# Decode index scores: keys as the moving side, queries as 32 weight columns, four matmuls on the four quarters of the array's columns

## The chip, the core and the metric

The kernel runs on one core of a Trainium2 chip. The metric is device time in microseconds (us) of one execution; lower is better. The engines of the core have these names in the profile: PE (TensorE, matmuls; PEld is its weight loads), DVE (VectorE), ACT (ScalarE), POOL (GpSimd) and SP (SyncE, which issues most DMAs). Each works through its own queue in order; semaphores tie them together.

## What is computed

One inference step of a hybrid decoder layer: a prompt of 1024 tokens and 8 decode sequences of one token each go through a common input projection, a sparse-attention head group, an mLSTM head group and an output projection. The change is in the sparse attention of the decode sequences. Each has 4096 past tokens in 32 pages of 128, scattered in a pool by a page table. An indexer scores every past key (64 numbers) against 16 query heads, and the best 256 tokens are then attended to:

```python
def indexer_scores(qi, ki, wi):
    s = jax.nn.relu(jnp.einsum('bqhd,bld->bqlh', qi, ki))
    return jnp.einsum('bqlh,bqh->bql', s, wi) * IDX_SCALE

def dsa_sample(q, k_new, v_new, qi, ki_new, wi, cache_k, cache_v, cache_ik, page_table):
    ki_past = cache_ik[page_table].reshape(Bd, past, IDX_DIM)
    ki_all = jnp.concatenate([ki_past, ki_new], axis=1)
    scores = indexer_scores(qi, ki_all, wi)
    ...
    _, idx = lax.top_k(scores, topk)
```

All in fp32. Only the order of the scores matters afterwards, so the kernel leaves the constant scale out.

## The kernel before

The kernel is one long stream of projection matmuls on PE, with everything else woven into it. The projections (`proj`, `mm` at L1410; `vproj` at L1479 and L1484) are computed in fp32r, each product split into high and low parts: three matmuls for one. Weights arrive as `wraw`, ACT casts the high part (L216, L1474) and DVE subtracts to get the low part (L217, L1475).

The other work is cut into jobs, Python generators that stand in two lanes (L1360). After each piece of a projection `lane.step` lets each lane advance; what a job `yield`s is a cost, and the lane spreads a job's total cost over the time up to the job's due end. So the yields set between which projection matmuls a job's instructions are written. A scheduler may then move instructions, except those that `pin` keeps in the order of the program. Every engine runs its queue in the order that comes out.

`job_dscore` is the first job of lane 1 and runs beside `vproj`, beside the first projections after it and beside lane 0's prompt indexer (`job_index`, L490 to L505). Its parts:

- The pool of indexer keys, `cik`, is laid out as rows (page, group of 4 dimensions), 2 KB each: 4 dimensions of 128 tokens. A gather (`fetch`, L996, an indirect DMA issued by POOL) brings 8 pages: partition 16g+q holds dimensions 4q to 4q+3 of page g. There are 4 gathers per batch, 32 in all, with 3 buffers `kp`. `idx` (L989) holds the row numbers.
- For each batch DVE builds `bd` (L1011): the queries, times a mask that is one only where page and column group agree.
- PE multiplies (L1016): weights are `kp[:, r, :]` (128 x 128 tokens), the moving side is `bd[:, r]` (128 columns: 8 pages by 16 heads), summed over r = 0 to 3. Four of these per gather, 16 per batch, 128 in all, fp32. The result has tokens on partitions and (page, head) on columns, in one bank for a batch's 32 pages.
- DVE applies relu and the head weights (`wib`) in one instruction (L1019) and adds over the 16 heads (L1021) into `sD`: token in page by (batch, page).
- At the end eight small matmuls (L1024) score the new keys.

`job_dsel` picks the best 256 from `sD`, and `job_datt` gathers and attends. PSUM has eight banks: three for the projections (`psj`), five that all others share (`bank()`).

Of the kernel before, what the change touches and what calls it, by code (L numbers as in the profile page):

```python
# [79 lines left out]
def constants():  # L80
# [8 lines left out]
    c[:, C_P64] = p % 16  # L89
# [52 lines left out]
def body(tc, A, stop=None):  # L142
# [830 lines left out]
    def job_dscore():  # L973
        with tc.tile_pool(name="ds", bufs=2, side="right") as pd:
            iqr = pd.tile([128, 4, 16, NB], F32, name="iqr", bufs=1)
            iqs = pd.tile([64, 16, NB], F32, name="iqs", bufs=1)
            g8 = pd.tile([128, 8], F32, name="g8", bufs=1)
            SY.dma_start(g8, A["cst"][:, C_G8:C_G8 + 8])
            wib = pd.tile([128, 16, NB], F32, name="wib", bufs=1)
            idx = pd.tile([128, 32], I32, name="idx", bufs=1)  # L980
            pte = pd.tile([128, 32], I32, name="pte", bufs=1)
            pin(SY.dma_start(pte, A["pte"]))
# [6 lines left out]
            pin(V.tensor_scalar(idx, pte, 16.0, cst[:, C_P64:C_P64 + 1], OP.mult, OP.add))  # L989
            V.memset(sD, NEG)  # L990
            kps = []

            def fetch(m):
                if m < NB * 4:
                    kp = pd.tile([128, 4, 128], F32, name="kp", bufs=3)
                    pin(G.indirect_dma_start(out=kp.rearrange("p r k -> p (r k)"), out_offset=None, in_=A["cik"],  # L996
                                             in_offset=bass.IndirectOffsetOnAxis(ap=idx[:, m:m + 1], axis=0)))
                    kps.append(kp)

            fetch(0)  # L1000
            yield 4
            fetch(1)
            yield 4
            for b in range(NB):
                ps = bank()
                for c in range(4):
                    fetch(b * 4 + c + 2)
                    if not c:
                        yield 2
                        bd = pd.tile([128, 4, 8, 16], F32, name="bd", bufs=1)  # L1010
                        pin(V.tensor_tensor(bd, iqr[:, :, :, b].unsqueeze(2).to_broadcast([128, 4, 8, 16]),  # L1011
                                            g8.unsqueeze(1).unsqueeze(3).to_broadcast([128, 4, 8, 16]), OP.mult))
                    yield 4 if c else 2
                    kp = kps.pop(0)
                    for r in range(4):
                        PE.matmul(ps[:, c * 128:c * 128 + 128], kp[:, r, :], bd[:, r].rearrange("p g h -> p (g h)"),  # L1016
                                  start=(r == 0), stop=(r == 3))
                tm = pd.tile([128, NPG, 16], F32, name="tm", bufs=1)
                V.scalar_tensor_tensor(tm, ps.rearrange("p (a h) -> p a h", h=16), 0.0,  # L1019
                                       wib[:, :, b].unsqueeze(1).to_broadcast([128, NPG, 16]), OP.max, OP.mult)  # L1020
                V.tensor_reduce(sD[:, b, 0:NPG], tm, AX.X, OP.add)  # L1021
            pn = bank()
            for b in range(NB):
                PE.matmul(pn[0:1, b * 16:b * 16 + 16], dec[0:64, T_MISC, b:b + 1], iqs[:, :, b], start=True, stop=True)  # L1024
# [377 lines left out]
    def mm(ps, cols, t, q, c, H, L, between={}):  # L1402
        c0, cn = chunks(t)[c]
        for k in range(4):
# [4 lines left out]
            for w_, x_, z in ((H, xH, 0), (H, xL, 1), (L, xH, 2)):  # L1409
                m = PE.matmul(ps[:cols, :cn], w_[:, k, :cols], x_[kk][:, c0:c0 + cn],  # L1410
                              start=(kk == 0 and z == 0), stop=(kk == 15 and z == 2))
                if k in between and z == 0:
                    pin(m)
# [362 lines left out]
```

## Time and profile before

| | |
|---|---|
| median of 3 runs | 2025.92 us (2025.28 to 2028.26) |
| the profiled execution | 2025.66 us, of which span 2023.9 us |
| granted TensorE clock, mean | 0.998 |
| decode score job, first and last matmul (L1016) | 203.8 and 418.6 us |

The span is the profiled part of an execution. In the lines below a group reads: line, engine, operation, output<-inputs by the program's names, shape, count, then durations. In a view of one line or tile the three numbers are least, median and greatest duration in ns, and the two after them the first and last start in us. In the timeline the two leading numbers are start and duration in us, and square brackets give the idle time of the engine just before and what ended it. A window row gives, for a stretch of time, each engine's busy time and instruction count, then the granted clock of PE, the DMA engines' busy share and GB/s. Matmuls are pipelined, so the records of PE overlap one another.

### The profile page before, as it was taken

The page shows a single profiled execution, that of the slowest core. Times are in us where ns is not written, and L with a number is a line of the kernel's source. Part 1 is how long each engine was busy: PE and PEld are TensorE (multiplying, and loading weights), DVE is VectorE, ACT ScalarE, POOL GpSimd, SP SyncE. Part 2 cuts the span into 40 slices and gives each one's busy share as a digit, 9 for nine tenths or more (in the row PEclk, how much of TensorE's full clock was granted, in tenths as well). Part 3 has the DMA queues.
Part 4 walks back from the last instruction along what each step waited for, and adds up shares of the span by engine and source line. Part 5 has one row for each costly group of instructions (what it writes and reads, how often), then busy time and mean ns, then how long its engine had stood idle before and what let it go on. Part 6 is the DMA issues. An engine that isn't in the chain of part 4 may idle for free.

```text
span 2023.9 us, 33968 instructions
## 1 busy us (share of the span) xinstructions
PE 2012.4 (99%) x12378; PEld 1925.2 (95%) x12378; DVE 1209.5 (60%) x3011; ACT 823.3 (41%) x1729; POOL 230.9 (11%) x295
## 2 busy tenths in 40 slices
PE   9999999999999999999999999999999999999998
PEld 9998999999999999999999999999999999988886
DVE  8333467756685876887455555436878556654332
ACT  8123345333531455312355555435555344423222
POOL 0000111100000000023110011012222211101110
PEclk9999999999999999999999999999999999999999
DMA  7444645432222212254422332145776658566212
GB/s 254 112 118 136 181 133 150 128 97 85 78 72 72 79 48 63 68 157 142 126 69 79 115 95 88 45 131 169 224 224 193 163 194 303 169 239 209 84 47 104
DMA packets 202004, 265.25 MB, mean 131 GB/s; under 512 B 33541, under 2 KB 128965, under 8 KB 201837
## 3 DMA queue, kind: packets, MB, share of 16 engines
q1 hardware_dynamic: 196589, 248.99, 40.2%
q0 software_dynamic: 4096, 12.59, 2.1%
q8 instruction: 97, 1.59, 0.3%
q10 hardware_dynamic: 1152, 1.51, 0.2%
q14 instruction: 70, 0.57, 0.1%
HBM read 203.19 MB, written 59.82 MB: 130 GB/s over the span
## 4 chain that ended last, share of the span: by engine, by line
PE 99%; issue 1%; DMA 0%; ACT 0%; DVE 0%; POOLq 0%; POOL 0%; SPq 0%; ACTq 0%
PE pj L1410 56%; PE bank L1601 7%; PE bank L1639 6%; PE pj L1639 4%; PE pj L1479 3%; PE bank L490 3%; PE pj L1484 3%; PE bank L686 3%; PE bank L635 3%; PE bank L1479 2%; PE bank L1410 2%; PE bank L677 2%; PE bank L1016 1%; PE bank L889 1%; PE bank L1484 1%
## 5 line engine op out<-in xcount | busy, mean ns | idle before, releaser
L1410 PE MATMUL pj<-xH,wH 128*128 128x344 f32 (+1 forms) x2352 | 759.6, 325 | 1.8 <-ACT xH L271 0.7
L1410 PE MATMUL pj<-xL,wH 128*128 128x344 f32 (+1 forms) x2352 | 761.1, 324 | 0.0
L1410 PE MATMUL pj<-xH,wL 128*128 128x344 f32 (+1 forms) x2352 | 758.7, 323 | 0.0
L1410 PEld LDWEIGHTS pj<-xH,wH 128*128 128x128 f32 x2352 | 443.0, 189 | 4.7 <-ACT xH L271 1.2
L1410 PEld LDWEIGHTS pj<-xL,wH 128*128 128x128 f32 x2352 | 443.0, 188 | 2.2 <-DVE xL L272 0.3
L1410 PEld LDWEIGHTS pj<-xH,wL 128*128 128x128 f32 x2352 | 443.3, 189 | 1.7
L216 ACT CAST wH<-wraw 128x512 fp32r<-128x512 f32 (+1 forms) x343 | 209.4, 615 | 515.2 <-PE pj L1410 313.1
L217 DVE TENSOR_TENSOR wL<-wraw,wH 128x512 fp32r<-128x512 f32 (+1 forms) x343 | 243.0, 715 | 292.6 <-ACT wH L216 285.0
L539 ACT ACTIVATE eq<-eq 128x512 bf16<-128x512 bf16 (+2 forms) x93 | 78.4, 843 | 97.1 <-DVE eq L538 97.0
L492 ACT ACTIVATE rl<-bank 128x512 f32<-128x512 f32 (+2 forms) x160 | 79.2, 523 | 89.9 <-PE bank L490 66.2
L495 DVE SCALAR_TENSOR_TENSOR s<-rl,wiN,s 128x512 f32<-128x512 f32 (+2 forms) x150 | 95.2, 656 | 29.9 <-ACT rl L492 28.3
L682 DVE TENSOR_TENSOR ptL<-bank,ptH 128x512 fp32r<-128x512 f32 (+1 forms) x80 | 50.5, 635 | 66.5 <-ACT ptH L681 65.8
L1601 PE MATMUL bank<-mL,wH 128*128 128x392 f32 x256 | 87.2, 341 | 0.0
L1601 PE MATMUL bank<-mH,wL 128*128 128x392 f32 x256 | 87.0, 341 | 0.0
L1601 PE MATMUL bank<-mH,wH 128*128 128x392 f32 x256 | 86.6, 341 | 0.0
L351 DVE TENSOR_TENSOR ev<-pj,rstd 128x344 f32<-128x344 f32 x120 | 61.4, 513 | 41.9 <-PE pj L1410 33.7
L490 PE MATMUL bank<-ki,qi 128*128 128x512 f32 (+2 forms) x320 | 78.2, 359 | 0.0
L1639 PE MATMUL bank<-wH,mH 128*128 128x512 f32 x192 | 75.5, 393 | 0.0
L1639 PE MATMUL bank<-wH,mL 128*128 128x512 f32 x192 | 75.3, 392 | 0.0
L1639 PE MATMUL bank<-wL,mH 128*128 128x512 f32 x192 | 75.2, 392 | 0.0
L1474 ACT CAST wH<-wraw 128x512 fp32r<-128x512 f32 (+1 forms) x64 | 38.6, 605 | 77.0 <-PE pj L1484 34.6
L681 ACT CAST ptH<-bank 128x512 fp32r<-128x512 f32 (+1 forms) x80 | 43.0, 541 | 65.3 <-PE bank L677 61.1
(438 smaller groups left out, 3439.7 us busy)
## 6 DMA issues: line engine op xcount, KB each, us to landing
wraw<-in_wa_dram SPq DMA_DIRECT2D x206, 256.0 KB
wraw<-in_wo_dram SPq DMA_DIRECT2D x64, 256.0 KB
wraw<-in_wt_dram SPq DMA_DIRECT2D x64, 256.0 KB
gateS<-ev SPq DMA_DIRECT2D x72, 172.0 KB
wraw<-in_wv_dram SPq DMA_DIRECT2D x32, 256.0 KB
qkv<-mlS SPq DMA_DIRECT2D x16, 512.0 KB
wraw<-in_wv_dram SPq DMA_DIRECT2D x32, 240.0 KB
xr<-in_xT_dram SPq DMA_DIRECT2D x14, 516.0 KB
```

The costliest lines, as they stand in the source:

```text
L216: a = SC.copy(H[:, s, :cols], raw[:, s, :cols])
L217: return a, V.tensor_tensor(L[:, s, :cols], raw[:, s, :cols], H[:, s, :cols].bitcast(F32), OP.subtract)
L351: v = V.tensor_tensor(e, ps[c][:cols, :cn], rstd[:cols, c0:c0 + cn], OP.mult)
L490: PE.matmul(p[:, :cn], qi[:, h % 4, :], ki[x][:, c0:c0 + cn], start=(x == 0), stop=(x == 1))
L492: SC.activation(r[:, :cn], p[:, :cn], AF.Relu)
L495: v = V.scalar_tensor_tensor(s[:, c0:c0 + cn], r[:, :cn], wv, s[:, c0:c0 + cn], OP.mult, OP.add)
L539: SC.activation(junk2[:, :W1], junk2[:, :W1], AF.Copy, accum_out=cnt[:, 1:2])
L1410: m = PE.matmul(ps[:cols, :cn], w_[:, k, :cols], x_[kk][:, c0:c0 + cn], start=(kk == 0 and z == 0), stop=(kk == 15 and z == 2))
L1479: PE.matmul(p[:, :nv], x_[:, b * 128:b * 128 + 128], w_, start=(n == 0 and z == 0), stop=(n == KT - 1 and z == 2))
L1484: PE.matmul(p[:j1 - j * 128, :cn], w_[:, j * 128:j1], x_[:, c0:R], start=(n == 0 and z == 0), stop=(n == KT - 1 and z == 2))
L1601: PE.matmul(p, w_[:, k, :], x_, start=(n == 0), stop=(n == 47))
L1639: PE.matmul(p, x_[:, bs], w_.rearrange("p a b -> p (a b)"), start=(n == 0 and z == 0), stop=(n == KT - 1 and z == 2))
```

## The change

The product is turned round: keys are now the moving side, and the queries are the weights.

- `cik` is laid out as rows (page, dimension) of 128 tokens, 512 bytes each. A gather brings two pages (64 dimensions each on the two halves of the partitions), and a buffer `kp` of 512 columns takes four gathers: 16 per batch, 128 in all, with 4 buffers. `idx` has 128 columns.
- `bd` is filled once by two DMAs, zero elsewhere: partitions 0 to 63 hold the queries for columns 0 to 15, partitions 64 to 127 for columns 16 to 31. Per batch DVE copies 32 columns of it to `st`.
- Per batch four matmuls with `st` as weights (32 columns) and a `kp` buffer as the moving side (512 columns) write to partitions 32j to 32j+31 of one bank, j in the order 3, 0, 1, 2. The rows are now (buffer j, half z, head), the columns (gather y, token).
- DVE does relu and head weight at once into `rf` (a fifth tenant of the four `kp` buffers); ACT and DVE split it into `rH` and `rL`. Two fp32r matmuls with a 0/1 matrix of 64 columns (`gz`, shifted by 8 per batch) add over heads, into rows 8b to 8b+7 of a bank `p2` that is held over all batches.
- At the end `p2` is copied, transposed in four pieces, and copied into `sD`.
- Some matmuls of the projections are pinned that were not, and eight small copies into `dec` move from POOL to DVE.

```diff
-            iqr = pd.tile([128, 4, 16, NB], F32, name="iqr", bufs=1)
...
+            bd = pd.tile([128, 2, 16, NB], F32, name="bd")
+            V.memset(bd, 0.0)
+            for z in range(2):
+                SY.dma_start(bd[z * 64:z * 64 + 64, z], iqD)
             for g in range(8):
-                SY.dma_start(iqr[g * 16:g * 16 + 16], iqD.rearrange("(q r) h b -> q r h b", r=4))
-            SY.dma_start(iqs, iqD)
-            SY.dma_start(wib, miscS[64:80, S:R].partition_broadcast(128))
+                SY.dma_start(wp[g * 16:g * 16 + 16], miscS[64:80, S:R])
+            SY.dma_start(w1, miscS[64:80, S:R].unsqueeze(0))
...
-            def fetch(m):
-                if m < NB * 4:
-                    kp = pd.tile([128, 4, 128], F32, name="kp", bufs=3)
-                    pin(G.indirect_dma_start(out=kp.rearrange("p r k -> p (r k)"), out_offset=None, in_=A["cik"],
+            def fetch(b, j):
+                kp = pd.tile([128, 4, 128], F32, name="kp", bufs=4)
+                for y in range(4):
+                    m = b * 16 + j * 4 + y
+                    pin(G.indirect_dma_start(out=kp[:, y, :], out_offset=None, in_=A["cik"],
                                              in_offset=bass.IndirectOffsetOnAxis(ap=idx[:, m:m + 1], axis=0)))
...
+            p2 = bank()[:64]
             for b in range(NB):
+                for j in range(4):
+                    if j:
+                        fetch(b, j)
+                    yield 7 if j == 3 else 3
                 ps = bank()
-                for c in range(4):
-                    fetch(b * 4 + c + 2)
-                    if not c:
-                        yield 2
-                        bd = pd.tile([128, 4, 8, 16], F32, name="bd", bufs=1)
-                        pin(V.tensor_tensor(bd, iqr[:, :, :, b].unsqueeze(2).to_broadcast([128, 4, 8, 16]),
-                                            g8.unsqueeze(1).unsqueeze(3).to_broadcast([128, 4, 8, 16]), OP.mult))
-                    yield 4 if c else 2
-                    kp = kps.pop(0)
-                    for r in range(4):
-                        PE.matmul(ps[:, c * 128:c * 128 + 128], kp[:, r, :], bd[:, r].rearrange("p g h -> p (g h)"),
-                                  start=(r == 0), stop=(r == 3))
-                tm = pd.tile([128, NPG, 16], F32, name="tm", bufs=1)
-                V.scalar_tensor_tensor(tm, ps.rearrange("p (a h) -> p a h", h=16), 0.0,
-                                       wib[:, :, b].unsqueeze(1).to_broadcast([128, NPG, 16]), OP.max, OP.mult)
-                V.tensor_reduce(sD[:, b, 0:NPG], tm, AX.X, OP.add)
+                st = pd.tile([128, 32], F32, name="st", bufs=1)
+                V.tensor_copy(st, bd[:, :, :, b].rearrange("p z h -> p (z h)"))
+                for j in (3, 0, 1, 2):
+                    pin(PE.matmul(ps[j * 32:j * 32 + 32, :], st, kps[j].rearrange("p y t -> p (y t)"), start=True, stop=True))
+                kps.clear()
+                rf = pd.tile([128, 4, 128], F32, name="kp", bufs=4).rearrange("p y t -> p (y t)")
+                V.tensor_scalar(rf, ps, 0.0, wp[:, b:b + 1], OP.max, OP.mult)
+                rH = pd.tile([128, 512], F32R, name="rH")
+                SC.copy(rH, rf)
+                rL = pd.tile([128, 512], F32R, name="rL")
+                V.tensor_tensor(rL, rf, rH.bitcast(F32), OP.subtract)
+                if b + 1 < NB:
+                    fetch(b + 1, 0)
+                gb = gz[:, 56 - 8 * b:120 - 8 * b]
+                PE.matmul(p2, gb, rH, start=(b == 0), stop=False)
+                PE.matmul(p2, gb, rL, start=False, stop=(b == NB - 1))
+            sT = pd.tile([128, 4, 128], F32, name="kp", bufs=4).rearrange("p y t -> p (y t)")[:64]
+            V.tensor_copy(sT, p2)
             pn = bank()
+            for y in range(4):
+                PE.transpose(pn[:, y * 64:y * 64 + 64], sT[:, y * 128:y * 128 + 128], ident[:64, :64])
+            for y in range(4):
+                V.tensor_copy(sD[:, :, 0:NPG].rearrange("p b (j y z) -> p y b j z", y=4, z=2)[:, y],
+                              pn[:, y * 64:y * 64 + 64].rearrange("p (b j z) -> p b j z", b=NB, z=2))
...
-                if k in between and z == 0:
+                if z == 0 and (k in between or t == T_AK and not k):
                     pin(m)
...
+                            if b == bs[0] and not z:
+                                pin(m)
...
-                                G.tensor_copy(dec[:m, T_MV + g * 4 + j, :], e[:m, S - t0:R - t0])
+                                V.tensor_copy(dec[:m, T_MV + g * 4 + j, :], e[:m, S - t0:R - t0])
...
-    a["cik"] = npa(cache_idx_k)[0].transpose(0, 2, 1).reshape(POOL * 16, 512)
+    a["cik"] = npa(cache_idx_k)[0].transpose(0, 2, 1).reshape(POOL * 64, 128)
```

More of the change, by code (lines that the diff above doesn't have):

```diff
@@ L973, in job_dscore @@
     def job_dscore():
-        with tc.tile_pool(name="ds", bufs=2, side="right") as pd:
-            iqr = pd.tile([128, 4, 16, NB], F32, name="iqr", bufs=1)
-            iqs = pd.tile([64, 16, NB], F32, name="iqs", bufs=1)
-            g8 = pd.tile([128, 8], F32, name="g8", bufs=1)
+        with tc.tile_pool(name="ds", bufs=1, side="right") as pd:
+            g8 = pd.tile([128, 8], F32, name="g8")
+            gz = pd.tile([128, 120], F32R, name="gz")
+            wp = pd.tile([128, NB], F32, name="wp")
+            w1 = pd.tile([1, 16, NB], F32, name="w1")
+            idx = pd.tile([128, NB * NPG // 2], I32, name="idx")
+            pin(SY.dma_start(idx, A["pte"]))
@@ L1028, in job_dscore @@
+            for b in range(NB):
+                PE.matmul(pn[0:1, 256 + b * 16:256 + b * 16 + 16], dec[0:64, T_MISC, b:b + 1], bd[0:64, 0, :, b],
+                          start=True, stop=True)
+            tn = pd.tile([1, NB, 16], F32, name="kp", bufs=4)
+            V.scalar_tensor_tensor(tn, pn[0:1, 256:384].rearrange("p (b h) -> p b h", h=16), 0.0,
+                                   w1.rearrange("p h b -> p b h"), OP.max, OP.mult)
             V.tensor_reduce(sD[0:1, :, NPG:NPG + 1], tn, AX.X, OP.add)
```

27 lines of the change are left out of this document (10 added, 17 removed).

## The prediction

> **What bounds the kernel now.** I read the page first, then the rows of the removed line, then PE's timeline around them. The page:
>
> ```profile
> span 2023.9 us, 33968 instructions
> PE 2012.4 (99%) x12378; PEld 1925.2 (95%) x12378; DVE 1209.5 (60%) x3011; ACT 823.3 (41%) x1729; POOL 230.9 (11%) x295
> PE 99%; issue 1%; DMA 0%; ACT 0%; DVE 0%; POOLq 0%; POOL 0%; SPq 0%; ACTq 0%
> ```
>
> PE is 99% of the span and 99% of the chain of waits. A microsecond of PE's stream taken out or put in is a microsecond of the result; work on DVE, ACT, POOL and SP counts only when PE waits for it. The score job, by its line and by the tile it gathers into:
>
> ```profile
> L1016 PEld LDWEIGHTS bank<-bd,kp x256: 186/192/193, 203.5 to 418.5; 128*128 128x128 f32 x128
> L1016 PE MATMUL bank<-bd,kp x256: 270/275/377, 203.8 to 418.6; 128*128 128x128 f32 x128
>   POOL kp L996: 163.1, 25
> DMA to landing us min/median/max: 3.2/3.8/6.2
> ```
>
> 128 fp32 matmuls leave 256 records: each is a weight load and a matmul, twice. Nobody on PE's side waits here: it is POOL that waited 163.1 us for PE to free a key buffer, so the gathers have run ahead of PE.
>
> **What goes.** A record's length is no price, because records overlap; the price is the step from start to start:
>
> ```profile
> 212.38 0.34 PE L1484 MATMUL pj<-xL,wH 128*128 128x392 f32 x1
> 212.56 0.34 PE L1484 MATMUL pj<-xH,wL 128*128 128x392 f32 x1
> 212.74 1.05 PE L1016 MATMUL bank<-bd,kp 128*128 128x128 f32 x8
> 213.55 0.48 PE L1479 MATMUL bank<-wH,xH 128*128 128x512 f32 x1
> 213.87 0.40 PE L1479 MATMUL bank<-wH,xL 128*128 128x512 f32 x1
> 214.11 0.40 PE L1479 MATMUL bank<-wL,xH 128*128 128x512 f32 x1
> ```
>
> From 212.74 to 213.87 are eight L1016 records and one 512-column matmul; the latter steps 0.23 to 0.24 us (213.87 to 214.11). So eight records hold PE 0.90 us, 0.11 each, and 32 such groups cost 28.8 us. A 392-column matmul steps 0.18.
>
> **What comes: the score matmuls.** Each of 8 batches gets four fp32 matmuls, 32 weight columns by 512 moving columns, on the four quarters of the array's columns. No row of before has an fp32 matmul that wide, so I price a record by how the step grows with the columns:
>
> ```profile
> 1378.49 0.31 PE L1186 MATMUL bank<-w,onesf 128*128 128x32 f32 x2
> 1378.63 0.60 PE L969 MATMUL bank<-cst,w 128*8 128x128 f32 x4
> 1573.54 0.33 PE L1229 MATMUL bank<-gi,onesf 128*128 128x64 f32 x2
> L969 PEld LDWEIGHTS bank<-cst,w x4: 87/88/170, 1378.5 to 1378.8; 128*8 128x8 f32 x4
> L969 PE MATMUL bank<-cst,w x4: 272/273/273, 1378.6 to 1379.0; 128*8 128x128 f32 x4
> ```
>
> A row of n records covers n-1 steps and one record of 0.27. That leaves 0.04 us at 32 columns, 0.06 at 64 and 0.11 at 128 (0.60 less 0.27, over 3). The step follows the moving columns, and L969 shows it with 8 weight columns, so the weight load does not make it. At 512 columns I estimate 4 x 0.108 = 0.43 us a record; it cannot well be under 0.23, the step of a 512-column fp32r matmul, nor over 4 x 0.11 = 0.44.
>
> Two records a matmul, four matmuls, 8 batches: 64 records. What they cost depends on whether two quarters stream at once, which no run here shows. Upper end, one after the other: 64 x 0.43 = 27.5 us, as much as what goes (the same products). Lower end, all four together: two records' time a batch, 8 x 0.86 = 6.9 us. In between, records start strictly in order: a quarter's second record must wait for its first, and the next quarter's first stands behind it in the queue, so only neighbours overlap (second record of one, first of the next). That is five record times a batch, 2.15 us, 17.2 us in all. I take this one: in every row above PE's records start in the order issued, and nothing in before overtakes.
>
> The Trainium skill's page "TensorE: Matmul & The Clock Gate" (Part 3) says that column tiles run at the same time, 2.38 times as fast for three, with matmuls in strict order of start and end. By 2.38 the sum of these records would be an estimated 11.6 us; by strict order with two records a matmul it is the 17.2 above. No run here shows it yet.
>
> Does a change of the array's shape cost? The nearest row is a matmul with 32 weight columns between full ones:
>
> ```profile
> 1149.52 0.32 PE L1410 MATMUL pj<-xL,wH 128*128 128x344 f32 x1
> 1149.68 0.32 PE L1410 MATMUL pj<-xH,wL 128*128 128x344 f32 x1
> 1149.84 0.28 PE L686 MATMUL bank<-ptH,vH 128*128 128x256 f32 x1
> 1149.95 0.27 PE L732 MATMUL bank<-cst,rc 128*32 128x128 f32 x1
> 1149.98 0.40 PE L1410 MATMUL pj<-xH,wH 128*128 128x344 f32 x1
> 1150.22 0.32 PE L1410 MATMUL pj<-xL,wH 128*128 128x344 f32 x1
> ```
>
> From 1149.95 to 1150.22 is 0.27 us: 0.11 for L732's 128 columns and 0.16 for L1410's 344, which is the ordinary step of the first two rows. Nothing is left for a switch, so I take none. The Trainium skill, "TensorEngine Tiling (Array Packing)" (Key Properties), says that a change of tiling mode drains the engine. If each of some 40 changes of shape drained for the 0.16 by which a 0.27 record outlasts its 0.11 step, an estimate of 6 us would be added; this row speaks against it.
>
> **What else PE gets.** 16 fp32r matmuls (L1029, L1030) of 512 columns, 0.23 each: 3.7 us. Four transposes at the end, at most 0.11 each: 0.5. The eight small matmuls with the new key stay.
>
> **The other engines.** DVE loses three instructions a batch, gets two large and a small one:
>
> ```profile
> L1011 DVE TENSOR_TENSOR bd<-iqr,g x8: 1145/1171/1215, 198.6 to 395.8; 128x512 f32<-128x512 f32 x8
> L1019 DVE SCALAR_TENSOR_TENSOR tm<-bank,wib x8: 1137/1166/1194, 221.4 to 419.2; 128x512 f32<-128x512 f32 x8
> L1021 DVE TENSOR_REDUCE sD<-tm x8: 668/685/702, 223.0 to 420.8; 128x32 f32<-128x512 f32 x8
> L217 DVE TENSOR_TENSOR wL<-wraw,wH 128x512 fp32r<-128x512 f32 (+1 forms) x343 | 243.0, 715 | 292.6 <-ACT wH L216 285.0
> L682 DVE TENSOR_TENSOR ptL<-bank,ptH 128x512 fp32r<-128x512 f32 (+1 forms) x80 | 50.5, 635 | 66.5 <-ACT ptH L681 65.8
> L681 ACT CAST ptH<-bank 128x512 fp32r<-128x512 f32 (+1 forms) x80 | 43.0, 541 | 65.3 <-PE bank L677 61.1
> ```
>
> 3.0 us a batch go; scaling out of the bank comes as L682 (0.64) and the low part as L217 (0.72), with ACT's cast 0.54. DVE is lighter, hidden either way at 60%. SP's issues stay at eleven, and eight small copies move from POOL to DVE: nothing under PE's cover. The bank of `p2` is held through all batches, but the one for scores now only for a moment, so the index job keeps two: nothing, while its relu empties them. But a new chain stands before PE: scores, DVE 0.64, ACT 0.54, then L1029, some 1.7 us with the 0.27 tail and hand-overs, more if a relu or a weight cast is ahead in either queue. In the built program's order 18 to 30 matmuls lie between in six batches (3 us or more, cover enough), 6 of them (1.4 us) in the second and 10 (2.3) in the seventh. I take 1.0 us of waiting in all; 0 to 4.
>
> **The gathers.** This is the change's weak place: one gather per four pages becomes one per page pair, 32 become 128. What POOL needs for one when nothing holds it back, from the attention job:
>
> ```profile
> 890.51 0.95 POOL L1258 DMA_INDIRECT kv<-in_ck_dram,idxs  x1 [0.30 <-DMA kv<-in_ck_dram,idxs]
> 891.76 0.95 POOL L1258 DMA_INDIRECT kv<-in_ck_dram,idxs  x1 [0.30 <-issue]
> 893.01 0.95 POOL L1258 DMA_INDIRECT kv<-in_ck_dram,idxs  x1 [0.30 <-issue]
> DMA to landing us min/median/max: 2.7/3.3/8.0
> 178.95 1.23 POOL L996 DMA_INDIRECT kp<-in_cik_dram,idx  x1 [7.00 <-DVE t L761]
> 180.49 0.95 POOL L996 DMA_INDIRECT kp<-in_cik_dram,idx  x1 [0.30 <-issue]
> ```
>
> 1.25 us from start to start, with 1 KB rows here and 0.95 also with the 2 KB rows of L996: it goes by gathers, not bytes. A batch's 16 gathers can begin when the batch before has freed its second buffer (2.0 us after its scores start, in the five-record case); the last is issued 15 x 1.25 = 18.75 us later and lands 3.3 to 3.8 us after that, say 3.5. Keys are complete 24.2 us after the last scores began, and the matmul that needs the last gather comes first (3, 0, 1, 2). PE meanwhile has, in the built order, between the second and third batch 55 matmuls of 512 columns and 36 of 392: 19.1 us, 21.3 with the scores. The next distances, likewise, are 25.3, 24.4, 24.9 and 23.2 (480 columns at 0.22, between the 0.18 of 392 and the 0.23 of 512); the first and last are over 35. PE waits 2.9 and 1.0: 3.9 us. Behind its wait stand all later matmuls; nothing overtakes. Bounds: nothing, if landing takes 2.7 and POOL 1.10; 24 us, if every gather took the 1.54 between the two L996 starts.
>
> A thin stretch can also halve the clock, as before shows after a run of tiny matmuls:
>
> ```profile
> 960.90:964.30 3.40, 3.40 (x14) 3.40 (x15) 0.00 (x0) 0.00 (x0) 2.63 (x4) 0.52 0.57 180
> 962.27 0.49 PE L1410 MATMUL pj<-xL,wH 128*128 128x344 f32 x1
> 962.55 0.49 PE L1410 MATMUL pj<-xH,wL 128*128 128x344 f32 x1
> ```
>
> Granted clock 0.52 over 3.4 us, steps 0.28 instead of 0.16, 12 of them: 1.6 us. A wait of 2.9 us may set it off once: I take half, 0.8.
>
> **Sum.** The profiled execution took 2025.66 us (span 2023.9, and 1.76 around it), 0.26 under the median 2025.92. 2025.66 - 28.8 + 17.2 + 3.7 + 0.5 + 3.9 + 1.0 + 0.8 = 2024.0.
>
> **Rivals.**
> Full overlap: four quarters together, both records. Scores cost 6.9; the gather wait grows to 5.2, because PE is back sooner (distances 20.0, 24.0, 23.1, 23.7, 21.9 against 23.4). 2024.0 - 10.3 + 1.3 = 2015.0. For it: quarters share no weights and no output rows. Against: each matmul's second record needs its own quarter again, in order.
> No overlap: the quarters take turns. Scores cost 27.5, the gather wait falls to 3.2: 2033.6, slower. The change then does not do what it says. For it: no row of before has two matmuls streaming at once. Against: nothing in the profile forbids it. The Trainium skill's page "TensorE: Matmul & The Clock Gate" (Part 3) lists that weight loads overlap running matmuls only where the row group differs, which would point here; in the L1016 rows loads of 0.19 and matmuls of 0.27 fit into steps of 0.11, so on the full array they do overlap.
> Slow gathers: five-record scores, but POOL, with DVE and the weight stream busy, needs more than 1.25 us a gather. From 1.35 it decides (waits 9.7, time 2029.7); at 1.40 the waits in the five tight stretches are 13.4 and the time is 2033.5. For it: the 1.23 record and the 1.54 step. Against: the run of even 1.25s.
>
> **Chances.** Five-record forecast 0.42, full overlap 0.21, no overlap 0.22, slow gathers 0.15. The forecast's own range, by its unknown waits, is 2018 to 2030. To hold 8 in 10 the range must reach both sides: 2013 to 2036. What a measurement of this kernel can tell from no change is about 0.2%, 4 us. Faster: full overlap and two fifths of the forecast, 0.37; within: half the forecast and crumbs, 0.24; slower: the rest, 0.39.
>
> **What would show it.** Score records starting 0.43 apart, with two running at once, about 2.2 us per batch from its first to the next other matmul: the forecast; 0.9 full overlap, 3.4 none. L1029 and L1030 stepping 0.23. PE idle before the third and seventh batch's scores, released by a gather into kp, 1 to 3 us each; POOL stepping 1.25 in rows of 16. If scores step otherwise than 0.43, or PE waits in more than those places, the sum is wrong there; if the order moved elsewhere costs PE new waits, it is wrong by what I left out.

## The result and the profile after

| | before | after |
|---|---|---|
| median of 5 runs each | 2026.97 us (2025.28 to 2028.26) | 2087.53 us (2080.61 to 2088.18) |
| ratio, 95% interval | | 1.0288 (1.0275 to 1.0301) |
| span of the profiled execution | 2023.9 us | 2086.2 us |
| granted TensorE clock, mean | 0.998 | 0.984 |

The change made the kernel 2.9% slower; the forecast was 2024.0 us, its range 2013 to 2036. The page of the changed kernel, from its first part, its 40 slices and its chain of waits:

```profile
span 2086.2 us, 33789 instructions
...
PE 2026.3 (97%) x12206; PEld 1913.6 (92%) x12206; DVE 1199.6 (58%) x3027; ACT 826.4 (40%) x1737; POOL 328.8 (16%) x383
...
PE   9999887889999999999999999999999999999998
...
PEclk9999998889999999999999999999999999999999
...
PE 92%; issue 3%; DVE 1%; another core or an unknown queue 1%; DMA 1%; ACT 1%; POOL 1%; SPq 0%; POOLq 0%; ACTq 0%; DVEq 0%
```

The loss lies in the fifth to ninth of the 40 slices, those of the score job: PE has holes there and the clock drops. "issue" and an unknown queue hold 4% of the chain now, against 1% before: time that the profile puts down to nothing it shows. First comes the part that went better than forecast, PE's timeline at the first batch's scores:

```profile
226.50 0.33 PE L1503 MATMUL pj<-xH,wL 128*128 128x392 f32 x1
226.76 1.06 PE L1018 MATMUL bank<-kp,st 128*32 128x512 f32 x8
227.75 0.45 PE L1503 MATMUL pj<-xH,wH 128*128 128x392 f32 x1
228.04 0.34 PE L1503 MATMUL pj<-xL,wH 128*128 128x392 f32 x1
```

From 226.76 to 227.75 is 0.99 us for all eight records. By the trace's start times the first records of all four quarters begin within 0.02 us of each other, and the four second ones 0.45 to 0.47 us after the first of all. This is full overlap. Counted as the prediction counted what goes, with the steps beside them, it is a little more: from 226.50 to 228.04 are 1.54 us, of which two 392-column matmuls take 0.18 each, so that a batch holds PE 1.18 us. Eight batches cost 9.4 us, where the forecast had 17.2. By that alone the sum falls to 2016.2 us; the result is 71 us above it.

The stretch of the job by windows, first of before, then of after (with the worst hole, what follows it and a quiet stretch). Behind the length stand busy time and count of PE, PEld, DVE, ACT and POOL, then PE's granted clock, the DMA share and GB/s. PE's longest waits of after, over the whole span, follow:

```profile
175.00:500.00 325.00, 325.00 (x1884) 302.36 (x1883) 204.87 (x508) 133.05 (x301) 35.50 (x43) 1.00 0.44 130
```

```profile
175.00:500.00 325.00, 278.23 (x1325) 233.14 (x1324) 154.78 (x417) 114.04 (x261) 130.91 (x129) 0.91 0.38 112
238.00:248.00 10.00, 3.52 (x19) 2.98 (x17) 0.62 (x1) 0.49 (x1) 7.56 (x9) 0.93 0.23 75
248.00:251.00 3.00, 0.00 (x0) 0.00 (x0) 0.00 (x0) 0.22 (x1) 0.15 (x1) 0.50 0.08 22
251.00:262.00 11.00, 10.68 (x42) 9.88 (x43) 5.52 (x9) 4.34 (x10) 0.00 (x0) 0.73 0.35 104
500.00:860.00 360.00, 360.00 (x2336) 347.83 (x2335) 252.75 (x708) 147.41 (x293) 6.71 (x14) 1.00 0.24 75
```

```profile
PE bank L490 <- ACT rl L492: 10.1, 2, 9.8
PE bank L1496 <- issue: 9.1, 5, 4.3
PE pj L1503 <- issue: 7.3, 9, 1.6
PE bank L1018 <- DMA kp<-in_cik_dram,idx: 5.9, 1, 5.9
PE pj L1496 <- issue: 4.0, 4, 2.0
```

PE is idle for 46.8 of 325 us, where before it never is, and the clock of 0.91 takes, as an estimate, another 0.09 x 278 = 25: together 72 us, about the whole of the 71. The low clock costs where PE works again behind a hole (0.73 from 251 to 262). The wait that the forecast feared, for a gather into `kp`, is one line of 5.9 us. The rest has no late transfer behind it. From 238 to 248 POOL is busy for 7.56 us, PE for 3.52, DVE and ACT for 0.62 and 0.49, and the DMA engines are at 0.23. The timeline of that hole:

```profile
237.20 0.95 POOL L999 DMA_INDIRECT kp<-in_cik_dram,idx  x1 [0.30 <-issue]
...
239.21 0.51 PE L490 MATMUL bank<-ki,qi 128*128 128x384 f32 x2
...
241.18 0.34 PE L1503 MATMUL bank<-xH,wL 128*128 128x392 f32 x1
242.21 0.95 POOL L999 DMA_INDIRECT kp<-in_cik_dram,idx  x1 [0.30 <-issue]
...
247.21 0.94 POOL L999 DMA_INDIRECT kp<-in_cik_dram,idx  x1 [0.30 <-issue]
250.78 0.38 SPq L472 DMA_DIRECT2D qi<-qS  x1
250.78 0.49 ACT L492 ACTIVATE rl<-bank 128x384 f32<-128x384 f32 x1 [12.24 <-remote]
...
251.31 0.62 DVE L495 SCALAR_TENSOR_TENSOR s<-rl,wiN,s 128x384 f32<-128x384 f32 x1 [12.11 <-ACT rl L492]
251.32 0.50 PEld L490 LDWEIGHTS bank<-ki,qi 128*128 128x128 f32 x2 [10.13 <-ACT rl L492]
251.32 1.01 PE L490 MATMUL bank<-ki,qi 128*128 128x384 f32 x2 [9.80 <-ACT rl L492]
```

Read it from the bottom. PE waits for ACT; DVE waits for ACT; and ACT's L492 waits for the bank that PE's L490 filled at 239.2 to 239.7. SP starts in the same moment as ACT. So what was late is the message that PE was done. The trace keeps the updates of PE's semaphore (number 102 here), in us from the start of the span:

```
PE's semaphore 102:        236.57  238.03  250.76  250.80  250.84  250.88  252.35
matmuls that raise it, start:      239.38  239.79  240.02  240.42
last gather's semaphore 118:               249.46 to 249.49
```

Four updates that should have come 0.3 us after 239.38 to 240.42 come 40 ns apart at 250.76, 1.3 us after the last gather of POOL's run of sixteen has landed. Count for each matmul that raises the semaphore, from 175 us to 15 us behind the last scores matmul, the first update recorded after its start. In before, none of the 258 comes later than 0.4 us after the start; in after, 57 of 275 come over 1 us after, the worst 11.5. (In after 252 updates are recorded for these 275 matmuls; one without a record of its own is counted with the next update, so the 57 is an upper bound.)

### The profile page after: what moved, and what is told of

Same layout as the page of the kernel before. It is cut to its first block, busy times and chain, and to the rows that moved or that the text cites. A ratio compares the mean times of both kernels' runs of the same rounds, so it can differ in the third digit from the quotient of the medians.

```text
span 2086.2 us, 33789 instructions
## 1 busy us (share of the span) xinstructions
PE 2026.3 (97%) x12206; PEld 1913.6 (92%) x12206; DVE 1199.6 (58%) x3027; ACT 826.4 (40%) x1737; POOL 328.8 (16%) x383
## 4 chain that ended last, share of the span: by engine, by line
PE 92%; issue 3%; DVE 1%; another core or an unknown queue 1%; DMA 1%; ACT 1%; POOL 1%; SPq 0%; POOLq 0%; ACTq 0%; DVEq 0%
PE pj L1427 54%; PE bank L1620 7%; PE bank L1658 6%; PE pj L1658 4%; PE bank L490 3%; PE bank L635 2%; PE bank L686 2%; PE pj L1496 2%; PE pj L1503 2%; PE bank L1427 2%; PE bank L1496 2%; PE bank L677 2%; PE bank L889 1%; PE bank L893 1%
## 5 line engine op out<-in xcount | busy, mean ns | idle before, releaser
L217 DVE TENSOR_TENSOR wL<-wraw,wH 128x512 fp32r<-128x512 f32 (+1 forms) x343 | 241.2, 710 | 292.2 <-ACT wH L216 277.6
L999 POOL DMA_INDIRECT kp<-in_cik_dram,idx x128 | 130.2, 1018 | 161.6 <-PE bank L1018 118.0
L492 ACT ACTIVATE rl<-bank 128x512 f32<-128x512 f32 (+2 forms) x160 | 78.8, 522 | 115.6 <-PE bank L490 72.9
L490 PE MATMUL bank<-ki,qi 128*128 128x512 f32 (+2 forms) x320 | 79.6, 367 | 14.3 <-ACT rl L492 10.1
L1492 DVE TENSOR_TENSOR wL<-wraw,wH 128x512 fp32r<-128x512 f32 (+1 forms) x64 | 42.6, 673 | 83.4 <-ACT wH L1491 49.0
L356 POOL COPY dec<-ev 128x8 f32<-128x8 f32 x20 | 10.1, 504 | 475.3 <-DVE ev L351 352.4
L490 PEld LDWEIGHTS bank<-ki,qi 128*128 128x128 f32 x320 | 55.7, 192 | 22.6 <-ACT rl L492 11.9
```

The source lines that it names most:

```text
L217: return a, V.tensor_tensor(L[:, s, :cols], raw[:, s, :cols], H[:, s, :cols].bitcast(F32), OP.subtract)
L490: PE.matmul(p[:, :cn], qi[:, h % 4, :], ki[x][:, c0:c0 + cn], start=(x == 0), stop=(x == 1))
L492: SC.activation(r[:, :cn], p[:, :cn], AF.Relu)
L999: pin(G.indirect_dma_start(out=kp[:, y, :], out_offset=None, in_=A["cik"], in_offset=bass.IndirectOffsetOnAxis(ap=idx[:, m:m + 1], axis=0)))
```

## The experiments

My theory A after this reading: POOL's runs of gathers delay the semaphores by which the other engines wait for one another. Rivals: PE's new order with its pins and the moved copies (B), the bytes or the short rows (C), the count of gathers (A2). Each ratio below is to before, measured in the same runs. The first four kernels:

**One gather per buffer instead of four.**

```diff
-                for y in range(4):
+                for y in range(1):
...
-                    ...(ps[j * 32:j * 32 + 32, :], st, kps[j].rearrange("p y t -> p (y t)"), ...)
+                    ...(ps[j * 32:j * 32 + 32, :], st, kps[j][:, 0:1].to_broadcast([128, 4, 128]), ...)
```

> The changed kernel with one gather for each key buffer instead of four: only the first quarter of each buffer is fetched and all four quarters of the matmul's moving side read it, so three quarters of the keys are left out; the matmuls, their sizes and everything on the other engines stay. POOL then issues 32 gathers instead of 128. Theory A (long back-to-back runs of gathers hold up the other engines): the holes of 1 to 10 us between 190 and 490 us are gone, and the time is the forecast's sum with the score matmuls at the 0.97 us per batch that the trace shows and no gather term: 2025.7 - 28.8 + 7.9 + 3.7 + 0.5 + 1.0 + 0.8 = 2010.8 us (2007 to 2016). Theory B (the holes come from PE's new order, the pinned matmuls or the dec copy on DVE, and the gathers only stand beside them): 2075 to 2090 us, as the changed kernel.

2017.49 us, ratio 0.9942 (0.9925 to 0.9958): theory A, 1.5 us above its range.

**Plain transfers on SP's queue.**

```diff
-                for y in range(4):
-                    m = b * 16 + j * 4 + y
-                    pin(G.indirect_dma_start(out=kp[:, y, :], ...))
+                m = (b * 4 + j) * 512
+                pin(SY.dma_start(kp, A["cik"][m:m + 512].rearrange("(p y) t -> p y t", y=4)))
```

> The changed kernel with the four gathers of each key buffer replaced by one plain transfer of the same 256 KB from fixed rows, in the same 512-byte pieces, issued on SP's queue; the page table is left out, so the keys are those of other pages. Theory A (it is POOL's gathers that hold up the other engines, not the bytes): about 2011 us, up to 2020 if SP's queue delays a weight transfer. Theory C (the 512-byte pieces or the bytes themselves starve other transfers): still 2060 to 2090 us. Theory B (PE's new order): 2075 to 2090 us.

2017.86 us, 0.9946 (0.9930 to 0.9963). Its window over the job, beside that of after above:

```profile
175.00:500.00 325.00, 323.12 (x1783) 288.15 (x1782) 198.94 (x527) 138.55 (x311) 2.26 (x4) 1.00 0.45 133
```

PE idles 1.9 us instead of 46.8 and the clock is whole, with all matmuls, pins and copies of the change in place and the same bytes arriving. B is out, and of C the bytes. The short rows are not out yet: the trace has these transfers in 4096 packets of 2 KB, not in the 512-byte pieces that the expectation names, so that rival waits for the plain transfers from POOL below. Over the whole span this kernel and after have the same 12206 records of PE; in after PE is busy 28.3 us longer for them (2026.3 against 1998.0) and idle 45.0 us longer, which makes up the difference of the two spans, 73.3 us. The new matmuls are worth 10.6 us (2028.49 - 2017.86) once the gathers are gone.

**Gathers released one by one.**

```diff
+                    i = idx[:, m:m + 1]
+                    pin(V.tensor_scalar(i, i, 64.0, cst[:, C_P64:C_P64 + 1], OP.mult, OP.add))
                     pin(G.indirect_dma_start(out=kp[:, y, :], ...))
+                    yield w
```

> The changed kernel with all 128 gathers, but each released by a small DVE instruction that makes its column of row numbers, and these spread over the steps of the job, so that gathers come one by one instead of 10 to 16 back to back. Theory A1 (the length of a run decides): 2011 to 2025 us. Theory A2 (each gather of 512-byte pieces costs the other engines its share, however it is spaced): 2060 to 2090 us. Theory B: 2075 to 2090 us.

(`w` is 0.8.) 2078.18 us, 1.0239 (1.0222 to 1.0256): inside the ranges of A2 and B and a miss for A1, but as the edit stood it did not pace. POOL's starts still form runs of up to 16, 15 and 13: once DVE itself is held up, its releases come in a heap.

**The kernel before with its gathers split in four.**

```diff
-                    pin(G.indirect_dma_start(out=kp.rearrange("p r k -> p (r k)"), ...
-                                             in_offset=...(ap=idx[:, m:m + 1], axis=0)))
+                    for r in range(4):
+                        pin(G.indirect_dma_start(out=kp[:, r, :], ...
+                                                 in_offset=...(ap=idx[:, r, m:m + 1], axis=0)))
```

> The kernel before with each of its 32 gathers of 2 KB rows split into four gathers of 512-byte rows: the same bytes and the same matmuls, runs of four gathers (5 us at 1.25 us each) with idle time between. Theory A1 (only long runs do harm): 2024 to 2032 us. Theory A2 (each gather costs, 60 us over 128 gathers): 2065 to 2085 us. Theory B (gathers are innocent): 2024 to 2028 us, with no late semaphore updates.

2051.76 us, 1.0109 (1.0086 to 1.0131), between A1 and A2. The old matmuls lose 23 us to the gathers alone. Of the 20.2 us in PE's steps over 0.65 us, 13.8 stand at two runs of twelve gathers (from 336 and 366 us); a third run of twelve, from 276 us, has 1.2 behind it, and twelve runs of exactly four have about 5 us of such steps behind them. So the run's length seems to matter more than the count, but a long run does not always cost.

The next four change the gathers' density and size.

**More time for the job; the same with gathers one by one; the same with POOL work between gathers.** Three kernels:

```diff
-             Lane([Job("dscore", T_MV, 18, 16 + 128 + 2, job_dscore),
+             Lane([Job("dscore", T_MV, 26, 16 + 128 + 2, job_dscore),
```

```diff
                     pin(G.indirect_dma_start(out=kp[:, y, :], ...))
+                    pin(G.tensor_tensor(gap, gap, mhalf.to_broadcast([128, 2]), OP.pow))
```

> The changed kernel with the scores job given until step 26 of the schedule instead of step 18, nothing else: the same gathers, twelve to sixteen back to back after each batch's scores, but batches farther apart. Theory A1 (long runs hold up the other engines, wherever they stand): 2065 to 2095 us, since each batch still has its run. Theory D (the job is only too dense: the gathers have too little time): 2013 to 2030 us. It is the control for the next two kernels.

> As the paced kernel (each gather released by a small DVE instruction of its own), with the scores job given until step 26 instead of step 18, so that there is about twice the time for each gather, some 4 us. Theory A1: runs stay at one to three gathers and the time falls to the level of the kernels without the gathers' load, 2012 to 2025 us, below the kernel before. Theory A2 (each gather costs its share, however spaced): 2060 to 2085 us.

> The changed kernel with the scores job given until step 26, and a 128x2 power on POOL (0.74 us each by the attention's rows of it) after every gather: runs stay twelve to sixteen gathers long, but one gather comes every 2.0 to 2.1 us instead of every 1.25. Theory E1 (the rate decides: gathers that follow each other at once hold up the others): 2015 to 2035 us. Theory E2 (the length of the run decides, its rate does not): 2065 to 2095 us.

2115.64, 2069.76 and 2060.86 us (1.0428, 1.0206, 1.0167). By time the first lies above A1's range, the second in A2's and the third between E1 and E2. But all three have a loss of their own: given until step 26, the job pushes what follows, and PE waits 25 to 29 us once, from 1655 us, 1661 or 1713. In the spaced kernel:

```profile
PE bank L1623 <- DMA mL<-gateS: 24.7, 1, 24.7
```

Inside the job they answer. PE's steps over 0.65 us sum to 46.3 us in 30 places in the control, to 5.5 in 5 with runs mostly of one to three gathers, and to 1.9 in 2 with runs of up to sixteen at 2.0 us each. So inside the job a run of sixteen does no such harm if it comes at 2.0 us a gather instead of 1.25: there E1 holds and E2 does not.

**Rows of 128 bytes.**

```diff
-                    pin(G.indirect_dma_start(out=kp[:, y, :], ...
+                    pin(G.indirect_dma_start(out=kp[:, y, :32], ...
```

> The changed kernel with the same 128 gathers of 128 rows each, but of 128-byte instead of 512-byte rows; the matmuls read each short row four times over, so three quarters of the keys are left out. Theory F1 (the gather's own work on POOL and its descriptors hold up the others): 2075 to 2095 us, as the changed kernel. Theory F2 (the bytes that the gathers move do): 2020 to 2050 us.

2097.02 us, 1.0336 (1.0294 to 1.0377), 2 us above F1's range: a quarter of the bytes, no less harm.

**The spaced kernel with less delay of the job, and with a shorter space** (`18` to `20`, `18` to `22`, and a multiply in place of the power with step 18 kept):

> All gathers, with the 0.74 us power on POOL after each (one gather every 2.05 us, as in the late spaced kernel, where PE's holes during the gathers were down to 1.5 us in all), but the scores job given until step 20 instead of 26, so that the waits of 25 to 30 us near 1655 us, which all three late kernels share, should stay away. A batch's 16 gathers take 32.8 us, about the 33 us that the schedule then leaves for a batch. Theory E1 (the rate of gathers is the whole loss): 2012 to 2024 us, faster than both kernels. Rival G (at this pace PE waits for the gathers instead): 2030 to 2055 us, with PE's waits at the scores matmuls ended by the transfer into kp.

> As the spaced kernel with step 20, with the job given until step 22: more time for the gathers of a batch, some 40 us, and less for what follows. Theory E1: 2012 to 2024 us if the later stages stay whole; if the wait near 1655 us grows with the shift in proportion (25 us for 8 steps), 2025 to 2035 us.

> The changed kernel with step 18 as it is, and a 128x2 multiply on POOL (0.26 us by the attention's rows) after each gather: one gather every 1.55 to 1.6 us instead of 1.25. Where the rate decides with a limit between 1.25 and 2.05 us, this tells on which side 1.6 lies: above the limit 2013 to 2025 us, below it 2050 to 2085 us. Where the loss is simply 128 gathers at a price each, 2080 to 2090 us.

2059.96 us (1.0157, 1.0129 to 1.0185), 2035.32 (1.0037, 1.0025 to 1.0049) and 2048.08 (1.0091, 1.0070 to 1.0113). None beats before. With step 20 the spaced gathers are too slow for the batches, as rival G has it, though the time is 5 us above G's range:

```profile
PE bank L1021 <- DMA kp<-in_cik_dram,idx: 17.0, 5, 9.0
```

These waits are half of the 34.5 us of PE's steps over 0.65 us in this job. With step 22 that wait is 6.1 us and PE's long steps sum to 10.0; the wait of 25 us near 1655 us stays away, and the time is just above the range that counted on it. The short space gave a step of 1.38 us rather than the 1.55 I had expected, and a result between the bounds: long steps of 32.2 us, of which 12.8 are waits for gathers. It shows no limit.

**The scores on the whole array.** Edit to the kernel with plain transfers (`st` is 224 columns wide, zero but for 96 to 127):

```diff
-                    pin(PE.matmul(ps[j * 32:j * 32 + 32, :], st, kps[j]..., start=True, stop=True))
+                    pin(PE.matmul(ps, st[:, 96 - 32 * j:224 - 32 * j], kps[j]..., start=n == 0, stop=n == 3))
```

> The kernel with plain transfers in place of the gathers (its own time 2017.9 us), with the four scores matmuls of a batch on the whole array instead of its four quarters: the 32 weight columns stand in a window of 128 columns with zeros beside them, and the four accumulate in one bank, so that the sums stay the same; the page table is left out here too. Theory H1 (the four quarters run at the same time, eight records in 0.97 us, and the whole array takes eight steps of 0.43 us, 3.4 us): 8 x 2.4 = 19 us more, 2037 us (2033 to 2041). Theory H2 (the order of the records, not the quarters, makes them short): 2016 to 2020 us.

2033.35 us, 1.0029 (1.0019 to 1.0039), 15.5 us more than the kernel that it edits, or 16.8 by the two ratios to before. PE's timeline at its first scores:

```profile
220.46 0.34 PE L1500 MATMUL pj<-xH,wL 128*128 128x392 f32 x1
220.64 3.60 PE L1014 MATMUL bank<-kp,st 128*128 128x512 f32 x8
223.67 0.75 PE L1500 MATMUL pj<-xH,wH 128*128 128x392 f32 x1
224.26 0.34 PE L1500 MATMUL pj<-xL,wH 128*128 128x392 f32 x1
```

The same eight records take 3.03 us to the next matmul's start instead of 0.99; with the steps beside them, 220.46 to 224.26 less two of 0.18, 3.44 instead of 1.18. Eight times the difference is 16.3 us by the first count and 18.1 by the second, and the time agrees with that size. H1: the quarters do run together, and the change does what it says.

**What in a gather does it.** Two kernels: gathers of 64 rows instead of 128 (the matmuls contract over 64 partitions), and plain transfers from POOL's own queue in the gathers' places:

```diff
-                    pin(G.indirect_dma_start(out=kp[:, y, :], out_offset=None, in_=A["cik"],
-                                             in_offset=bass.IndirectOffsetOnAxis(ap=idx[:, m:m + 1], axis=0)))
+                    pin(G.dma_start(kp[:, y, :], A["cik"][m * 128:m * 128 + 128]))
```

> The changed kernel with its 128 gathers, each of 64 rows instead of 128: the scores matmuls contract over the lower 64 partitions alone, so every second page is left out. Theory I1 (each row's descriptors count): half the rows, so less than half of the loss of 70 us over the kernel with plain transfers is left: 2020 to 2050 us, and a gather may step faster than 1.25 us. Theory I2 (the gather instruction as such counts): 2070 to 2095 us, step 1.25 us.

> The changed kernel with 128 plain transfers of 128 rows of 512 bytes issued by POOL in the gathers' places, from fixed rows; the page table is left out. Theory J1 (POOL writing a descriptor for each row, looked up or not, holds up the others): 2060 to 2095 us. Theory J2 (the lookup of the rows does): 2012 to 2025 us.

2099.92 us (1.0358, 1.0343 to 1.0374), 5 us above I2's range with a step of 1.21 us, and 2018.01 us (0.9950, 0.9935 to 0.9965), J2. Half the rows do as much harm; the same number of rows and bytes without the lookup does none. The page's row of POOL's queue (packets, MB, share) and its group of the line (busy us, mean ns, idle before), first of after and then of the plain transfers from POOL:

```profile
q0 software_dynamic: 5632, 12.59, 2.0%
...
L999 POOL DMA_INDIRECT kp<-in_cik_dram,idx x128 | 130.2, 1018 | 161.6 <-PE bank L1018 118.0
```

```profile
q0 software_dynamic: 5632, 12.59, 2.1%
...
L999 POOL DMA_DIRECT2D kp<-in_cik_dram x128 | 68.5, 545 | 144.1 <-PE bank L1017 141.3
```

Equal packets, equal bytes, the same queue, sixteen in a row too: that puts out the short rows as well, the rest of C. What differs is that POOL takes 1.02 us on the mean for one that looks its rows up and 0.55 for one that does not, and that only with the first kind PE's semaphore is late. The table counts as above:

| kernel | transfers of POOL in the job | PE's updates over 1 us late in the job, worst | PE's steps over 0.65 us in the job |
|---|---|---|---|
| before | 32 gathers | 0 of 258 | none |
| after | 128 gathers | 57 of 275, 11.5 us | 59.2 us |
| one gather per buffer | 32 gathers | 3 of 280, 3.0 us | 3.4 us |
| before, gathers split | 128 gathers | 65 of 353, 10.5 us | 20.2 us |
| short rows | 128 gathers | 65 of 277, 14.8 us | 71.5 us |
| half the rows | 128 gathers | 65 of 275, 14.7 us | 69.0 us |
| one by one, step 26 | 128 gathers | 39 of 394, 11.6 us | 5.5 us |
| spaced, step 26 | 128 gathers | 11 of 390, 8.0 us | 1.9 us |
| plain from SP | none | 0 of 277 | 2.2 us |
| plain from POOL | 128 plain | 0 of 277 | 2.1 us |

Wherever gathers run, the third column is an upper bound. In the two kernels with step 26 only 338 and 354 updates are recorded for the 394 and 390 matmuls; how many of their late ones are real is not settled, but PE hardly waits there.

**The right keys without lookups on POOL.** Page numbers in registers, 64 rows a transfer, 256 transfers: all from SP; every other from POOL, with step 18 and with step 20; and 214 from POOL with 42 from SP:

```diff
+                    for z, E in enumerate((G, SY)):
+                        page = E.value_load(idx[z * 64:z * 64 + 1, m:m + 1])
+                        pin(E.dma_start(kp[z * 64:z * 64 + 64, y, :], A["cik"][bass.ds(page * 64, 64)]))
```

> The changed kernel with the same pages of the page table, but each page (64 rows of 512 bytes) fetched by a transfer of SP's, with the page's number loaded into a register: 256 transfers on SP's queue and none of the gathers on POOL. Theory A: as with plain transfers, 2014 to 2020 us, faster than both kernels by some 0.4%. Rival K (a register load and a transfer take SP about 1 us or more together, so SP's queue is late with weights and keys): 2030 to 2100 us, with PE's waits ended by transfers into wraw or kp.

> The changed kernel with the pages fetched by plain transfers with the page's number in a register, every other page from POOL's queue and every other from SP's: 16 transfers for a batch on each at 1.42 us (SP's step with all 32), 22.7 us, where batches stand 28 to 31 us apart. Theory A: 2014 to 2024 us, faster than both kernels. Rival K (SP's own transfers, behind 1.42 us each, come late, or POOL's step is longer): 2030 to 2080 us, PE's waits ended by transfers into kp or wraw.

> The same with the scores job given until step 20 of the schedule instead of 18: some 33 us for a batch, and so more room on both queues. Theory A: 2014 to 2026 us; a few us more than with step 18 if that one has no late transfers, less if it has. Rival K: 2030 to 2060 us.

> As the kernel with two queues (2041.3 us), but POOL issues 214 of the 256 plain transfers with the page's number in a register and SP only 42, none of them for the first batch. POOL steps 0.95 us in the kernel with two queues, so a batch's 26 take 24.7 us, inside the 28 to 31 us between batches; SP's queue loses 6 x 1.0 us a batch instead of 16, and its first weights of the job are no longer 5 us late. Theory A: 2015 to 2024 us, faster than the kernel before. Rival K: 2028 to 2045 us, with weights of SP's queue or the last keys of a batch still late.

2217.86, 2041.32, 2053.69 and 2071.30 us (1.0929, 1.0069, 1.0130, 1.0224): rival K each time, the first and the last beyond its range. SP alone steps 1.42 us a transfer, and PE waits for keys:

```profile
PE bank L1018 <- DMA kp<-in_cik_dram: 112.3, 6, 36.0
```

With two queues none of PE's 280 updates is late, though these transfers read the same scattered pages as the gathers: the scatter is not what holds the semaphore up. But the weights on SP's queue are late; ACT's wait for them in the job, first with two queues and then with plain transfers:

```profile
ACT wH L1491 <- DMA wraw<-in_wv_dram: 24.4, 8, 5.4
```

```profile
ACT wH L1489 <- DMA wraw<-in_wv_dram: 7.2, 5, 2.3
```

With most on POOL, its step was 1.12 us instead of the 0.95 I had counted on, so a batch's 26 take 29 us, and PE waited 30.9 us for keys. In it runs of 26 transfers at 1.12 us last longer than sixteen gathers at 1.25, and the worst of PE's updates in the job is 1.1 us late: it is not how long POOL issues without a break either. No kernel that fetches the table's pages beat the kernel before; the gain of some 10 us stands only in kernels whose keys are of fixed rows or partly left out.

## Why the prediction was wrong

- *What goes* (28.8 us): nothing contradicts it. With the quarters at 9.4 the sum without gather waits is 2012.3 us, 13.6 below before; the kernels with plain transfers or a quarter of the gathers stand 10.2 to 11.0 below theirs. The 3 us between were not traced.
- *What comes, the five-record case* (17.2 us): mis-sized. The step of 0.43 us held, as the whole array shows. The queueing argument did not: a quarter's second record does not hold up the first of the next quarter, since all four first records begin within 0.02 us. A batch takes 1.18 us instead of 2.15, so 9.4 us in all. Full overlap, given 0.21, is what happened to this term. The rule of the Trainium skill's page "TensorE: Matmul & The Clock Gate" (Part 3) that column tiles run at the same time agrees with the trace: 3.44 us on the whole array against 1.18 on four quarters, 2.9 times, where the page has 2.38 for three.
- *No cost for the change of shape*: a little too low. A batch's 1.18 us are 0.32 more than two record steps of 0.43, 2.6 us in all, and 0.08 of the 0.32 lies in the step into the scores (0.26 instead of 0.18). The Trainium skill's page "TensorEngine Tiling (Array Packing)" (Key Properties) says that a change of tiling mode drains the engine; whether that is what these 0.32 us are, no run here shows.
- *L1029 and L1030*: 0.23 us a step as forecast.
- *The gathers*: the rates were right, 1.25 us a step and rows of sixteen, and the wait at the third batch's scores came, 5.9 us instead of 2.9; the seventh's did not. The step that failed is the frame around it: "work on DVE, ACT, POOL and SP counts only when PE waits for it", with POOL's gathers mattering through `kp` alone. The runs showed POOL's lookups holding up PE's semaphore, and with it every engine that waits for PE and then PE itself: 45.0 us of idle PE and, at a lowered clock, 28.3 us of longer work, with transfers that but for one wait of 5.9 us were in time.
- *The clock* (0.8 us): mis-sized by some 25 us. The low clock stands in and behind the holes; the windows give 0.93, 0.50 and 0.73 around one of them.
- *Rivals*: slow gathers (0.15) blamed the right instruction with the wrong mechanism: gathers at an even 1.25 us did the harm, and it was not through late keys. The last sentence of the prediction, new waits from the order moved elsewhere, is refuted by the plain kernels, which have that order.

Before gives hardly a warning. Its score job's gathers come singly or in groups of at most three. The attention job's gathers, the ones I took the 1.25 us from and read for POOL's rate alone, come in unbroken runs of at most five there, and no update by PE among them is over 1 us late. In the kernel with plain transfers from POOL, whose score job has no gathers, a trace of the effect stands at the same attention job: the only updates by PE that come over 1 us late in the whole span, five of them and by at most 2.5 us, belong to matmuls at 893 to 969 us, among those gathers (890.6 to 975.5).

## What to carry to other kernels

When a change multiplies the indirect transfers of one engine, look at how they will bunch and ask what the other engines' signals do meanwhile; a share of busy time of 16% says nothing about that. Where waits are put down to "issue" or an unknown queue on several engines at once, compare the time at which the producer finished with the time at which its semaphore rose. And before redesigning the transfers, replace them by plain ones from fixed rows: two such runs priced both halves of this change.

## What the runs showed of the hardware that was not expected

- Four fp32 matmuls of 32 weight columns on the four column quarters start within 20 ns of each other and take 0.99 us for eight records of 512 columns to the next matmul's start, where the whole array takes 3.03 (1.18 and 3.44 with the steps beside them).
- Back-to-back indirect transfers of POOL (1.25 us a step) make PE's semaphore updates up to 11.5 us late in after and up to 14.8 with short rows, and held updates then arrive 40 ns apart (250.76 to 250.88 us in after). (DVE's and ACT's records are too incomplete in these runs to say the same of theirs.) It happens with 512-byte and 128-byte rows and with 128 and 64 rows, little in runs of four, and not with plain transfers of the same packets at 0.55 us. At a step of 2.0 us it costs PE hardly anything in the job (long steps of 1.9 us). That the indirect form is the condition is shown; through which path it holds up the semaphores is open.
- A page number in a register costs: SP's step with load and transfer is 1.42 us where all are on it; POOL's was 0.95 with half of them and 1.12 with most.
